# A hybrid encoder trunk on one core: one PSUM ring of four instead of two rings of two, the retention branch put in another order, and column sums issued behind projections

## The chip, the cores and the metric

The kernel runs on 1 core of one Trainium2 chip. The metric is the device time in microseconds of a whole execution, in one launch. Beside it stands the profile of one execution, whose span runs from the first to the last instruction of the program.

## The reference

Two layers (DEPTH = 2) work on 528 tokens (16 learned ones in front of 512) of width 1024, in float32. Each layer does this:

```python
h = h + token_mixer(rms_norm(h, norm_mix[i]), w_in[i], conv_w[i], ...)
h = h + swiglu(rms_norm(h, norm_ffn[i]), w_ffn_in[i], w_ffn_out[i])
```

The mixer projects h by w_in to 12,320 columns and feeds two branches. The gated DeltaNet branch (8 heads of 128) runs a short convolution, normalises q and k, and runs a chunked recurrence in both directions. The retention branch (4 heads, q and k of 256, v of 512) rotates q and k, and adds `gamma^|n-m| (q_n . k_m)` times v over all tokens, forwards and backwards. Each branch's output is divided by its root mean square per head and token, multiplied by a silu gate, and projected up (w_up_a, w_up_b); two sigmoid gates merge them, and w_out gives the mixer's result. The feed-forward part is silu(gate) times up (2816 wide) and a projection back. A last root-mean-square norm drops the 16 learned tokens.

## The kernel before, in words

**Data.** Activations lie with channels on the 128 partitions and tokens along the free axis. Float32 products are made from two reduced-precision parts: a matrix is split into a high and a low tile (`split`, L178: a cast on ScalarE, then a subtraction on VectorE), and `mm3` issues three matmuls for each 128 x 128 block: high x high, high x low, low x high.

**A projection unit** (`project`, L419; `units` calls it and yields) makes 128 output channels: it loads 512 KB of weights on SyncE's DMA queue, splits them, takes PSUM tiles for its token stretches, and issues 24 matmuls for each. In layer 0 the stretches are two of 264 tokens (FULL), so a unit holds two PSUM tiles; in layer 1 many units need only the 512 real tokens (TAIL), one tile. Then `consume` empties each tile on ScalarE or VectorE (a copy for q, k, v; a tanh and a product for gates).

**PSUM** has eight banks of one tile each, in three rings: `pmm` (two, for projection units), `pmx` (two, taken by `pt`, for scores, transposes, products with v, and column sums), and `pmc` (four, taken by `ct`, for the DeltaNet chain and the first units after a norm).

**The mixer.** For each of four pairs of DeltaNet heads, `gdn_begin` makes the projections and convolutions, and `gdn_chain` the recurrence: many small matmuls, each waiting for the step before it on VectorE or ScalarE, and some round trips through DRAM (the tiles nd, w, xd, qc). `weave` (L1042) alternates the steps of the chain with a `filling` generator: three retention heads, gates, and z projections. Each step yields a cost, and `weave` takes as much of the one as of the other by these costs (NA, NB). The fourth retention head comes after all chains (L1075).

**A retention head** (L930) builds a strip of decays, makes q and k (four units, the tiles rp0 and rp1, then the rotation to `rot`), runs other filler, makes the scores of five chunks of keys (`rs` in PSUM, times the strip to `pr`, split to `prh` and `prl`), and then for each of four blocks dv of value channels: one unit for the values (`rvc`), their transposes (`rvt`, `rvm`, split to `rv` and `vst`), one unit for the gate (`rg`), and the product of scores and values (`rpv`: 13 matmuls for each token stretch), emptied by a square (`rsq`) and a product with the gate (`ro`), which goes to DRAM (od_b).

**Column sums of squares** (`mean_square`, L823): two small matmuls with a column of ones (`oms`) for each stretch, on tiles split from the squares (osh and osl of DeltaNet, prh and prl of retention). They are put into the list `later` and given out by `sums`: in the second head's part of `gdn_begin`, ahead of the retention filler, and at the mixer's end. Their rows go to DRAM and come back (`ir`) as inverse roots.

**What follows the mixer** is `project` for w_up_a (emptied by `mrg`), w_up_b, w_out, the feed-forward part, each with weights split on the way. `residual` and `first_units` treat the last and first units at a norm in their own order. In the last layer `done` and `laid` transpose the output (`ops`) as its channels come.

**Order.** The program gives the instructions out in the order of the code; a scheduler at build time then orders each engine's queue by priority, by its own estimate of when each is ready, and by the tiles of a ring that are free (`high_priority` moves some ahead). `issue_after(i)` keeps an instruction behind instruction i on the same engine's queue. On the chip each queue then runs as written. `newest[0]` is the last matmul given out.

Of the kernel before, what the change touches and what calls it, by code (L numbers as in the profile page):

```python
# [9 lines left out]
F32 = mybir.dt.float32  # L10
# [8 lines left out]
P = 128  # L19
# [27 lines left out]
OA = 1000  # L47
OB = 300
UB = 6
TB = 4  # L50

TCKW = dict(schedule_with_timeline_sim=True)
PRI = 200
# [44 lines left out]
def trunk(ctx: ExitStack, tc: tile.TileContext, x, meta, norm_mix, w_in, conv_w, a_log, dt_bias, gdn_norm,  # L98
# [4 lines left out]
    wp = ctx.enter_context(tc.tile_pool(name="wp", bufs=2))  # L103
    xp = ctx.enter_context(tc.tile_pool(name="xp", bufs=1))
    tp = ctx.enter_context(tc.tile_pool(name="tp", bufs=TB))
    pmm = ctx.enter_context(tc.tile_pool(name="pmm", bufs=2, space=PSUM))
    pmx = ctx.enter_context(tc.tile_pool(name="pmx", bufs=2, space=PSUM))
    pmc = ctx.enter_context(tc.tile_pool(name="pmc", bufs=4, space=PSUM))

    newest = [None]  # L110
# [21 lines left out]
        return tp.tile([P, L + 4], F32, name=name, tag="u", bufs=UB)  # L132

    def pt(name="px"):
        return pmx.tile([P, 512], F32, name=name, tag="mx")

    def ct(name="pc"):
        return pmc.tile([P, 512], F32, name=name, tag="mc")
# [163 lines left out]
    with tc.tile_pool(name="ip", bufs=1) as ip:  # L302
        xt = ip.tile([P, NCH, D], F32, name="xt")
        xs_ = ip.tile([P, NCH, D], F32, name="xs")
        raw = tp.tile([42, P], F32, name="gr", tag="t")
        ss = ip.tile([P, NCH], F32, name="ss")
        nc.vector.memset(ss, 1.0)
        act(ss[0:1, 0:1], ss[0:1, 0:1], AF.Square)
        nc.sync.dma_start(xt[0:NM, NC], meta)
        nc.sync.dma_start(xt[:, 0], x[0, 0:P, :])  # L310
        nc.sync.dma_start(xt[:, 1], x[0, P:2 * P, :])
        nc.sync.dma_start(raw[0:16, :], norm_mix.rearrange("l (i p) -> (l i) p", p=P))
        nc.sync.dma_start(raw[16:32, :], norm_ffn.rearrange("l (i p) -> (l i) p", p=P))
        nc.sync.dma_start(raw[32:40, :], norm_final.rearrange("(i p) -> i p", p=P))
        nc.sync.dma_start(raw[40:42, :], gdn_norm)
        ps = pt()
        nc.tensor.transpose(ps[:, :42], raw, ident[:42, :42])
        nc.vector.tensor_copy(gain, ps[:, :42])
        xn = xtiles()
        PARTS = ((NC, 0, 1), (2, 3))  # L320
        warm = pt("warm")
        for _ in range(WU):
            nc.tensor.transpose(warm[:, 0:P], ident, ident)
        SPAN = ((0, 272), (272, 256))

        def turned(i):
            return pmm.tile([P, 512], F32, name="lay", tag="mm") if i % 2 else pt("lay")

        def lay(src, i, part, ps):
            o = 0  # L330
            for c in PARTS[part]:
                n = NM if c == NC else P
                nc.tensor.transpose(ps[:, o:o + n], src[0:n, c, i * P:(i + 1) * P], ident[:n, :n])
                o += n

        def normed(part):
            for c in PARTS[part]:
                n = NM if c == NC else P
                if c == NC:
                    tt(xs_[0:n, c], xt[0:n, c], xt[0:n, c], MUL)  # L340
                    nc.vector.tensor_reduce(out=ss[0:n, c:c + 1], in_=xs_[0:n, c], op=ADD, axis=AX.X)
                else:
                    act(xs_[0:n, c], xt[0:n, c], AF.Square, accum_out=ss[0:n, c:c + 1])
            ms = tp.tile([P, 66], F32, name="ms0", tag="nw", bufs=3)[:, 0:NCH]
            ts(ms, ss, 1.0 / D, MUL, s2=EPS, op2=ADD)
            rs = inverse_root(ms, NCH)
            for c in PARTS[part]:
                n = NM if c == NC else P
                ts(xs_[0:n, c], xt[0:n, c], rs[0:n, c:c + 1], MUL)
            n0, n = SPAN[part]  # L350
            for i in range(KT):
                ps = turned(i)
                lay(xs_, i, part, ps)
                h, lo = xn[0][i][:, n0:n0 + n], xn[1][i][:, n0:n0 + n]
                a = nc.scalar.activation(h, ps[:, :n], AF.Copy, scale=gain[:, i:i + 1])
                b = nc.vector.scalar_tensor_tensor(out=lo, in0=ps[:, :n], scalar=gain[:, i:i + 1], in1=h.bitcast(F32), op0=MUL, op1=SUB)
                if part:
                    behind[:] = a.ins, b.ins

        def before(j):  # L360
            if j == 0:
                for c in (2, 3):
                    nc.sync.dma_start(xt[:, c], x[0, c * P:(c + 1) * P, :])
            normed(j)

        gd = first_gates(0, xn, FULL, before=before, late=True)
# [34 lines left out]
def layer(tc, nc, env, l, xn, gd):  # L401
# [14 lines left out]
    def acc(tiles):  # L416
        return lambda k: tiles[k]

    def project(src, c0, nt, xs, halves, consume, kts=(8,)):  # L419

        xh, xl = xs
        for t in range(nt):
            pss = [pmm.tile([P, 512], F32, name="mmps", tag="mm") for _ in halves]
            k0 = 0
            for j, kt in enumerate(kts):
                w = weights(src[k0 * P:(k0 + kt) * P], c0 + t * P, kt)
                for (n0, n), ps in zip(halves, pss):
                    mm3(ps, w, acc(xh), acc(xl), kt, n0, n, first=j == 0, last=j == len(kts) - 1, k0=k0)
                k0 += kt
            for (n0, n), ps in zip(halves, pss):  # L430
                consume(t, n0, n, ps[:, :n])
# [391 lines left out]
    def mean_square(row, sq, scale, bias, ms, pt):  # L823

        ms = ms[0:1]
        for n0, n in tail:
            ps = pt("oms")
            for j in range(2):
                mm(ps[0:1, :n], one, sq[j][:, n0:n0 + n], start=j == 0, stop=j == 1)
            act(ms[:, n0:n0 + n], ps[0:1, :n], AF.Copy, scale=scale, bias=bias)  # L830
        nc.sync.dma_start(msd[row:row + 1, :], ms[:, t0:L])

# [39 lines left out]
    def gdn_begin(gi, st):  # L872
        hs = (2 * gi, 2 * gi + 1)
        st["ssk"] = gp.tile([P, 2, NCH], F32, name="ssk", tag="ssk")
        nc.vector.memset(st["ssk"], 0.0)
        st["w0"] = gp.tile([68, 1024], F32, name="w0", tag="w0", bufs=1)
        sc = iter(())
        for h in hs:
            for y in gdn_front(h, st):
                next(sc, None)  # L880
                yield y
                if h == hs[1]:
                    sums(ct)
                lead[0] = PRI
            if gi == 0 and h == 0:
                sc = scalars()
                next(sc)
        for _ in sc:
            pass
        sums(ct)  # L890
# [39 lines left out]
    def retention(h, filler):  # L930
# [30 lines left out]
        sums(pt)  # L961
        yield from filler
        pr = []
        for c in range(NCH):
            m0, m = tok(c)
            o = tmp("pr")
            base = 400 - m0
# [10 lines left out]
            else:  # L978
                split(pst[0:NM, t0:L], pst[32:32 + NM, t0:L], o[0:NM, t0:L])
                nc.scalar.copy(pst[64:64 + NM, t0:L], pst[0:NM, t0:L].bitcast(F32))  # L980
            yield 1.8
        sqa = rp.tile([P, SW], F32, name="rsq", tag="strip")[:, 0:L]
        for dv in range(4):
            vc = tmp("rvc")

            def consume(t, n0, n, ps):
                nc.scalar.copy(vc[:, n0:n0 + n], ps)
            yield from units(W, C_VB + h * DV + dv * P, 1, xn, FULL, consume)
            rv = rp.tile([P, 2, NC * P], F32R, name="rv", tag="rot", bufs=2)
            vh, vl = rv[:, 0], rv[:, 1]  # L990
            vst = vsts[dv % 2]
# [6 lines left out]
            nc.tensor.transpose(pm[0:NM, 0:P], vc[:, 0:NM], ident)  # L998
            split(vst[0:NM], vst[64:64 + NM], pm[0:NM, 0:P])
            nc.scalar.copy(vst[32:32 + NM], vst[0:NM].bitcast(F32))  # L1000
            gs = tmp("rg")
            yield from units(W, C_GB + h * DV + dv * P, 1, xn, tail, gated(gs))
            o = tmp("ro")
            sq = sqa if dv == 0 else tmp("rsq2")
            for n0, n in tail:
                ps = pt("rpv")
                for c in range(NC):
                    for a, b in ((vh, 0), (vh, 1), (vl, 0)):
                        mm(ps[:, :n], a[:, c * P:(c + 1) * P], pr[c][b][:, n0:n0 + n], start=c + b == 0 and a is vh, stop=False)
                mm(ps[:, :n], vst, pst[:, n0:n0 + n], start=False)  # L1010
                act(sq[:, n0:n0 + n], ps[:, :n], AF.Square)
                tt(o[:, n0:n0 + n], ps[:, :n], gs[:, n0:n0 + n], MUL)
            nc.sync.dma_start(od_b[h * 4 + dv, :, t0:L], o[:, t0:L])
            if dv:
                tt(sqa[:, t0:L], sqa[:, t0:L], sq[:, t0:L], ADD)
            yield 4.5
        sq = [rp.tile([P, L], F32R, name=n, tag=n, bufs=4) for n in ("prh", "prl")]
        split(sq[0][:, t0:L], sq[1][:, t0:L], sqa[:, t0:L])
        later.append(lambda ps: mean_square(H + h, sq, 4.0 / DV, 4 * 256 * EPS, tmp("ms"), ps))

    def merge_gates(i0, i1):
# [54 lines left out]
        pass  # L1076
    sums(pt)
    mixctx.close()

    bctx = ExitStack()  # L1080
    b0 = bctx.enter_context(tc.tile_pool(name=f"b0{l}", bufs=1, reuse_waits="tile"))
# [186 lines left out]
    def done(i, h, n0, n):  # L1268
# [8 lines left out]
        if i == 7 and n0 > NM:  # L1277
            laid(i, h, n0, n)
            finish(n0, n)
        elif i < 7:  # L1280
            laid(i, h, n0, n)
        else:
            half.append((i, h, n0, n))

    half = []

# [49 lines left out]
```

## Time and profile before

| | us |
|---|---|
| median of 3 runs | 2948.24 (2946.37 to 2952.17) |
| the profiled execution | 2948.52 |
| its span | 2946.7 |
| PE busy in it | 2831.8 |
| DVE busy | 1802.9 |
| ACT busy | 1103.0 |

PE is TensorE's matmul stream, PEld its weight loads, DVE VectorE, ACT ScalarE. Busy time is the union of an engine's instructions. The projections (tile mmps) hold most of it. The mixer of layer 0 runs to about 915 us and its dense part to 1503 us; the mixer of layer 1 runs from about 1530 to 2385 us.

### The profile page before, as it was taken

The numbers are of one execution on the slowest core, as the hardware profiler recorded it, in microseconds if no ns is written. First come the engines' busy times: TensorE is split into PE (matmuls) and PEld (weight loads), VectorE is DVE, ScalarE is ACT, GpSimd is POOL, SyncE is SP. The second block draws the span as 40 slices with busy tenths as digits, with TensorE's granted clock in tenths as the row PEclk, the third lists the DMA queues.
The fourth block names the chain that finished last, engine by engine and source line by source line (L and its number), as shares of the span: only waits on it lengthen the run. The fifth ranks groups of instructions, "written<-read, shape, count | busy, mean of one in ns | idle before, by whom it ended". The sixth has DMA issues, their size and how long they took to land.

```text
span 2946.7 us, 48876 instructions
## 1 busy us (share of the span) xinstructions
PE 2831.8 (96%) x19487; PEld 2574.8 (87%) x19487; DVE 1802.9 (61%) x3854; ACT 1103.0 (37%) x2171; POOL 9.0 (0%) x114
## 2 busy tenths in 40 slices
PE   8999999999989999999999899999999999999998
PEld 8899998899979999999998797887888778888887
DVE  6867968778565445433358768687785654543333
ACT  5434444344333233222244343443444332332222
POOL 0000000000000000000000000000000000000000
PEclk9999999999999999999999999999999999999999
DMA  6322323234345442333444323334243464433332
GB/s 165 104 80 77 105 77 105 73 78 118 87 147 167 128 142 84 89 93 95 120 116 109 103 68 96 87 83 108 70 118 94 144 188 121 127 108 98 94 107 81
DMA packets 506423, 313.49 MB, mean 106 GB/s; under 512 B 55632, under 2 KB 460778, under 8 KB 506194
## 3 DMA queue, kind: packets, MB, share of 16 engines
q1 hardware_dynamic: 506194, 310.36, 37.1%
q8 instruction: 153, 2.51, 0.4%
q14 instruction: 76, 0.62, 0.1%
HBM read 265.28 MB, written 45.02 MB: 105 GB/s over the span
## 4 chain that ended last, share of the span: by engine, by line
PE 80%; DVE 10%; DMA 6%; ACT 3%; issue 1%; SPq 1%; DVEq 0%; ACTq 0%
PE mmps L113 64%; PE rpv L113 3%; PE oo L113 2%; PE fu L113 1%; DVE wlo L180 1%; PE rs L113 1%; PE sn L113 1%; PE yy L113 1%; DMA lo<-od_a 1%; ACT whi L179 1%; PE ks L113 1%; DMA xd<-w 1%; DVE N L116 1%; DMA gcr<-grow 1%; DMA nd<-NT 1%
## 5 line engine op out<-in xcount | busy, mean ns | idle before, releaser
L113 PE MATMUL mmps<-xh,whi 128*128 128x264 f32 (+1 forms) x3840 | 1195.8, 312 | 24.2 <-ACT rp L946 12.3
L113 PE MATMUL mmps<-xl,whi 128*128 128x264 f32 (+1 forms) x3840 | 1184.9, 309 | 0.0
L113 PE MATMUL mmps<-xh,wlo 128*128 128x264 f32 (+1 forms) x3808 | 1178.6, 310 | 0.5 <-DVE wlo L180 0.5
L113 PEld LDWEIGHTS mmps<-xh,whi 128*128 128x128 f32 x3840 | 730.0, 190 | 69.2 <-ACT rp L946 13.6
L113 PEld LDWEIGHTS mmps<-xl,whi 128*128 128x128 f32 x3840 | 729.3, 190 | 38.3 <-issue 4.0
L113 PEld LDWEIGHTS mmps<-xh,wlo 128*128 128x128 f32 x3808 | 722.6, 190 | 36.8 <-issue 2.3
L180 DVE TENSOR_TENSOR wlo<-wraw,whi 128x1024 fp32r<-128x1024 f32 (+1 forms) x392 | 474.4, 1211 | 457.4 <-ACT whi L179 455.1
L179 ACT CAST whi<-wraw 128x1024 fp32r<-128x1024 f32 (+1 forms) x392 | 408.3, 1042 | 888.9 <-PE mmps L113 667.6
L113 PE MATMUL mmps<-oh,whi 128*128 128x264 f32 (+2 forms) x1126 | 359.2, 319 | 7.2 <-DVE mrg L116 7.0
L113 PE MATMUL mmps<-ol,whi 128*128 128x264 f32 (+2 forms) x1126 | 358.4, 318 | 0.0
L113 PE MATMUL mmps<-oh,wlo 128*128 128x264 f32 (+2 forms) x1126 | 358.0, 318 | 0.0
L113 PEld LDWEIGHTS mmps<-oh,whi 128*128 128x128 f32 x1126 | 211.7, 188 | 24.1 <-DVE mrg L116 5.5
L113 PEld LDWEIGHTS mmps<-oh,wlo 128*128 128x128 f32 x1126 | 211.9, 188 | 15.7
L113 PEld LDWEIGHTS mmps<-ol,whi 128*128 128x128 f32 x1126 | 211.7, 188 | 15.2
L116 DVE SCALAR_TENSOR_TENSOR ac<-xc,cw,ac 128x528 f32<-128x528 f32 x192 | 146.4, 763 | 6.9 <-ACT ac L126 1.4
L119 DVE TENSOR_TENSOR ff<-fg,mmps 128x264 f32<-128x264 f32 (+1 forms) x63 | 32.4, 515 | 115.7 <-PE mmps L113 115.7
L113 PE MATMUL rpv<-prh,rv 128*128 128x264 f32 (+1 forms) x384 | 96.0, 324 | 1.7 <-DVE rv L180 1.7
L113 PE MATMUL rs<-rot 128*128 128x264 f32 (+3 forms) x240 | 82.2, 475 | 11.5 <-DVE pr L119 8.7
L119 DVE TENSOR_TENSOR st<-w 68x30 f32<-68x30 f32 (+14 forms) x240 | 78.2, 326 | 23.1 <-DMA w<-ndm 10.3
L126 ACT ACTIVATE gth<-mmps 128x264 f32<-128x264 f32 (+1 forms) x132 | 60.0, 454 | 61.1 <-PE mmps L113 61.0
L119 DVE TENSOR_TENSOR w<-w,st 68x30 f32<-68x30 f32 (+14 forms) x240 | 78.1, 326 | 6.7
L116 DVE SCALAR_TENSOR_TENSOR hn<-mmps,hold 128x264 f32<-128x264 f32 (+2 forms) x51 | 25.3, 498 | 76.9 <-PE mmps L113 70.9
(315 smaller groups left out, 3191.6 us busy)
## 6 DMA issues: line engine op xcount, KB each, us to landing
wraw<-in_w_in_dram SPq DMA_DIRECT2D x194, 512.0 KB
wraw<-in_w_ffn_in_dram SPq DMA_DIRECT2D x88, 512.0 KB
wraw<-in_w_up_b_dram SPq DMA_DIRECT2D x32, 512.0 KB
wraw<-in_w_ffn_out_dram SPq DMA_DIRECT2D x32, 512.0 KB
gcr<-grow SPq DMA_DIRECT2D x32, 264.0 KB
wraw<-in_w_up_a_dram SPq DMA_DIRECT2D x16, 512.0 KB
wraw<-in_w_out_dram SPq DMA_DIRECT2D x16, 512.0 KB
wraw<-in_w_ffn_out_dram SPq DMA_DIRECT2D x16, 384.0 KB
```

The source lines that it names most:

```text
L113: newest[0] = nc.tensor.matmul(o, lhsT=l, rhs=r, start=start, stop=stop)
L116: (eng or nc.vector).scalar_tensor_tensor(out=o, in0=a, scalar=s, in1=b, op0=op0, op1=op1)
L119: (eng or nc.vector).tensor_tensor(out=o, in0=a, in1=b, op=op)
L126: nc.scalar.activation(o, a, f, **kw)
L179: a = nc.scalar.copy(hi, src)
L180: return a.ins, nc.vector.tensor_tensor(out=lo, in0=src, in1=hi.bitcast(F32), op=SUB).ins
```

## The change

- The rings `pmm` and `pmx` become one ring of four (`pmm`), from which both `project` and `pt` take tiles; `turned` takes all of its tiles from it.
- After a layer's mixer (`wide[0] = 1`) `project` takes the tiles of one unit from `pmc` and those of the next from `pmm` in turn.
- A retention head gives out its value unit and its gate unit for block 0 among the scores (after chunks 1 and 3), and then, for each block, the values of block dv, the product of block dv - 1, the transposes of block dv, and the gate of block dv. The cost that a product yields is 3.2 and not 4.5.
- `mean_square` keeps its matmuls behind the newest matmul given out, and `gdn_begin` gives out the sums one step later.
- In the last layer `done` transposes a block when the next has come, the pool of temporary tiles `t` has six places and not four, and the DMA scratch size is 1024 and not 2048.

```diff
--- before.py
+++ after.py
@@ -47,7 +47,7 @@
 OA = 1000
 OB = 300
 UB = 6
-TB = 4
+TB = 6
 
 TCKW = dict(schedule_with_timeline_sim=True)
 PRI = 200
@@ -103,8 +103,7 @@
     wp = ctx.enter_context(tc.tile_pool(name="wp", bufs=2))
     xp = ctx.enter_context(tc.tile_pool(name="xp", bufs=1))
     tp = ctx.enter_context(tc.tile_pool(name="tp", bufs=TB))
-    pmm = ctx.enter_context(tc.tile_pool(name="pmm", bufs=2, space=PSUM))
-    pmx = ctx.enter_context(tc.tile_pool(name="pmx", bufs=2, space=PSUM))
+    pmm = ctx.enter_context(tc.tile_pool(name="pmm", bufs=4, space=PSUM))
     pmc = ctx.enter_context(tc.tile_pool(name="pmc", bufs=4, space=PSUM))
 
     newest = [None]
@@ -132,7 +131,7 @@
         return tp.tile([P, L + 4], F32, name=name, tag="u", bufs=UB)
 
     def pt(name="px"):
-        return pmx.tile([P, 512], F32, name=name, tag="mx")
+        return pmm.tile([P, 512], F32, name=name, tag="mm")
 
     def ct(name="pc"):
         return pmc.tile([P, 512], F32, name=name, tag="mc")
@@ -324,7 +323,7 @@
         SPAN = ((0, 272), (272, 256))
 
         def turned(i):
-            return pmm.tile([P, 512], F32, name="lay", tag="mm") if i % 2 else pt("lay")
+            return pt("lay")
 
         def lay(src, i, part, ps):
             o = 0
@@ -416,11 +415,15 @@
     def acc(tiles):
         return lambda k: tiles[k]
 
+
+    wide = [0]
+
     def project(src, c0, nt, xs, halves, consume, kts=(8,)):
 
         xh, xl = xs
         for t in range(nt):
-            pss = [pmm.tile([P, 512], F32, name="mmps", tag="mm") for _ in halves]
+            wide[0] += wide[0] > 0
+            pss = [(ct if wide[0] % 2 else pt)("mmps") for _ in halves]
             k0 = 0
             for j, kt in enumerate(kts):
                 w = weights(src[k0 * P:(k0 + kt) * P], c0 + t * P, kt)
@@ -825,8 +828,9 @@
         ms = ms[0:1]
         for n0, n in tail:
             ps = pt("oms")
-            for j in range(2):
-                mm(ps[0:1, :n], one, sq[j][:, n0:n0 + n], start=j == 0, stop=j == 1)
+            with tc.issue_after(newest[0].ins):
+                for j in range(2):
+                    mm(ps[0:1, :n], one, sq[j][:, n0:n0 + n], start=j == 0, stop=j == 1)
             act(ms[:, n0:n0 + n], ps[0:1, :n], AF.Copy, scale=scale, bias=bias)
         nc.sync.dma_start(msd[row:row + 1, :], ms[:, t0:L])
 
@@ -875,12 +879,15 @@
         nc.vector.memset(st["ssk"], 0.0)
         st["w0"] = gp.tile([68, 1024], F32, name="w0", tag="w0", bufs=1)
         sc = iter(())
+        turns = 0
         for h in hs:
             for y in gdn_front(h, st):
                 next(sc, None)
                 yield y
                 if h == hs[1]:
-                    sums(ct)
+                    turns += 1
+                    if turns > 1:
+                        sums(ct)
                 lead[0] = PRI
             if gi == 0 and h == 0:
                 sc = scalars()
@@ -961,7 +968,8 @@
         sums(pt)
         yield from filler
         pr = []
-        for c in range(NCH):
+
+        def scores(c):
             m0, m = tok(c)
             o = tmp("pr")
             base = 400 - m0
@@ -978,14 +986,23 @@
             else:
                 split(pst[0:NM, t0:L], pst[32:32 + NM, t0:L], o[0:NM, t0:L])
                 nc.scalar.copy(pst[64:64 + NM, t0:L], pst[0:NM, t0:L].bitcast(F32))
-            yield 1.8
-        sqa = rp.tile([P, SW], F32, name="rsq", tag="strip")[:, 0:L]
-        for dv in range(4):
-            vc = tmp("rvc")
+
+        V, G, S = {}, {}, []
+
+        def values(dv):
+            V[dv] = tmp("rvc")
 
             def consume(t, n0, n, ps):
-                nc.scalar.copy(vc[:, n0:n0 + n], ps)
+                nc.scalar.copy(V[dv][:, n0:n0 + n], ps)
             yield from units(W, C_VB + h * DV + dv * P, 1, xn, FULL, consume)
+
+        def gates(dv):
+            G[dv] = tmp("rg")
+            yield from units(W, C_GB + h * DV + dv * P, 1, xn, tail, gated(G[dv]))
+
+        def turn(dv):
+
+            vc = V[dv]
             rv = rp.tile([P, 2, NC * P], F32R, name="rv", tag="rot", bufs=2)
             vh, vl = rv[:, 0], rv[:, 1]
             vst = vsts[dv % 2]
@@ -998,10 +1015,13 @@
             nc.tensor.transpose(pm[0:NM, 0:P], vc[:, 0:NM], ident)
             split(vst[0:NM], vst[64:64 + NM], pm[0:NM, 0:P])
             nc.scalar.copy(vst[32:32 + NM], vst[0:NM].bitcast(F32))
-            gs = tmp("rg")
-            yield from units(W, C_GB + h * DV + dv * P, 1, xn, tail, gated(gs))
+            V[dv] = vh, vl, vst
+
+        def weighted(dv):
+            vh, vl, vst = V[dv]
             o = tmp("ro")
-            sq = sqa if dv == 0 else tmp("rsq2")
+            sq = tmp("rsq2") if S else rp.tile([P, SW], F32, name="rsq", tag="strip")[:, 0:L]
+            S.append(sq)
             for n0, n in tail:
                 ps = pt("rpv")
                 for c in range(NC):
@@ -1009,13 +1029,30 @@
                         mm(ps[:, :n], a[:, c * P:(c + 1) * P], pr[c][b][:, n0:n0 + n], start=c + b == 0 and a is vh, stop=False)
                 mm(ps[:, :n], vst, pst[:, n0:n0 + n], start=False)
                 act(sq[:, n0:n0 + n], ps[:, :n], AF.Square)
-                tt(o[:, n0:n0 + n], ps[:, :n], gs[:, n0:n0 + n], MUL)
+                tt(o[:, n0:n0 + n], ps[:, :n], G[dv][:, n0:n0 + n], MUL)
             nc.sync.dma_start(od_b[h * 4 + dv, :, t0:L], o[:, t0:L])
             if dv:
-                tt(sqa[:, t0:L], sqa[:, t0:L], sq[:, t0:L], ADD)
-            yield 4.5
+                tt(S[0][:, t0:L], S[0][:, t0:L], sq[:, t0:L], ADD)
+
+
+        for c in range(NCH):
+            scores(c)
+            yield 1.8
+            if c == 1:
+                yield from values(0)
+            if c == 3:
+                yield from gates(0)
+        turn(0)
+        for dv in range(1, 5):
+            if dv < 4:
+                yield from values(dv)
+            weighted(dv - 1)
+            yield 3.2
+            if dv < 4:
+                turn(dv)
+                yield from gates(dv)
         sq = [rp.tile([P, L], F32R, name=n, tag=n, bufs=4) for n in ("prh", "prl")]
-        split(sq[0][:, t0:L], sq[1][:, t0:L], sqa[:, t0:L])
+        split(sq[0][:, t0:L], sq[1][:, t0:L], S[0][:, t0:L])
         later.append(lambda ps: mean_square(H + h, sq, 4.0 / DV, 4 * 256 * EPS, tmp("ms"), ps))
 
     def merge_gates(i0, i1):
@@ -1076,6 +1113,7 @@
         pass
     sums(pt)
     mixctx.close()
+    wide[0] = 1
 
     bctx = ExitStack()
     b0 = bctx.enter_context(tc.tile_pool(name=f"b0{l}", bufs=1, reuse_waits="tile"))
@@ -1277,10 +1315,10 @@
         if i == 7 and n0 > NM:
             laid(i, h, n0, n)
             finish(n0, n)
-        elif i < 7:
-            laid(i, h, n0, n)
-        else:
-            half.append((i, h, n0, n))
+            return
+        while half:
+            laid(*half.pop())
+        half.append((i, h, n0, n))
 
     half = []
 
@@ -1322,7 +1360,7 @@
     import concourse.bacc as bacc
     from concourse.bass_utils import run_bass_kernel_spmd as run
 
-    nc = bacc.Bacc("TRN2", target_bir_lowering=False, num_devices=1, dynamic_dma_scratch_size=2048)
+    nc = bacc.Bacc("TRN2", target_bir_lowering=False, num_devices=1, dynamic_dma_scratch_size=1024)
     arrays, args = {}, []
     given = [(n, np.ascontiguousarray(inputs[n])) for n in _INS] + [("const", CONST)]
     for name, a in given:
```

## Rows read from the trace of the kernel before

**Rows 1.** The page: busy time, share of the span and instructions of each engine.

```profile
PE 2831.8 (96%) x19487; PEld 2574.8 (87%) x19487; DVE 1802.9 (61%) x3854; ACT 1103.0 (37%) x2171; POOL 9.0 (0%) x114
```

**Rows 2.** Both mixers: window, length, busy of PE, PEld, DVE, ACT, POOL; clock; DMA.

```profile
65.00:925.00 860.00, 819.28 (x6510) 778.57 (x6509) 623.69 (x1508) 361.45 (x832) 3.19 (x44) 0.98 0.35 96
...
1590.00:2310.00 720.00, 684.78 (x4388) 589.55 (x4387) 536.86 (x1299) 304.97 (x666) 2.89 (x40) 0.99 0.34 91
```

**Rows 3.** The chain that ended last, dense stretch: start, length, what.

```profile
1139.04 363.74 PE mmps L113 x2978
```

**Rows 4.** Who waited for whom, PE: total, times, longest.

```profile
PE mmps L113 <- ACT rp L946: 12.3, 6, 4.8
...
PE rs L113 <- DVE pr L119: 8.7, 6, 3.5
PE lvy L113 <- DVE QT L119: 8.1, 5, 3.5
...
PE rvt L995 <- ACT rvc L987: 7.1, 6, 1.7
PE mmps L113 <- DVE mrg L116: 7.0, 3, 2.4
PE mmps L113 <- ACT xc L538: 6.8, 9, 1.5
PE oms L113 <- ACT osh L179: 6.5, 7, 2.2
PE mmps L113 <- DVE rg L116: 3.5, 4, 1.7
PE rvt L995 <- DVE w L119: 3.1, 1, 3.1
...
PE oms L113 <- ACT prh L179: 2.7, 1, 2.7
PE oms L113 <- DVE prl L180: 1.8, 3, 0.9
PE rpv L113 <- DVE rv L180: 1.7, 3, 0.8
PE oms L113 <- DVE osl L180: 1.6, 4, 0.4
```

**Rows 5.** ACT in order of time at the longest projection wait: start, length, instruction.

```profile
517.14 0.98 ACT L126 ACTIVATE strip<-strip 128x928 f32<-128x928 f32 x1 [9.41 <-DVE strip L116]
518.02 0.36 ACT L946 COPY rp<-mmps 128x264 f32<-128x264 f32 x1
```

**Rows 6.** Products emptied, slowest and last case: start, length, instruction.

```profile
190.59 0.29 PE L113 MATMUL rpv<-pst,vst 96*128 96x264 f32 x1
...
195.69 0.43 DVE L119 TENSOR_TENSOR ro<-rpv,rg 128x264 f32<-128x264 f32 x1
...
910.26 0.29 PE L113 MATMUL rpv<-pst,vst 96*128 96x264 f32 x1
...
911.01 0.43 DVE L119 TENSOR_TENSOR ro<-rpv,rg 128x264 f32<-128x264 f32 x1 [0.21 <-ACT rsq L126]
```

**Rows 7.** Who waited for whom, DVE for DMA: total, times, longest.

```profile
DVE qd L683 <- DMA qc<-xd: 26.3, 7, 5.3
...
DVE dm L116 <- DMA gcr<-grow: 12.6, 12, 1.9
...
DVE st L119 <- DMA w<-ndm: 10.3, 6, 3.8
```

**Rows 8.** Column sums at the last chain's end, each layer: busy, mean ns, idle before.

```profile
L113 PE MATMUL oms<-osh,one 128*1 128x264 f32 x4 | 1.0, 342 | 2.4 <-ACT osh L179 2.4
...
L113 PE MATMUL oms<-osh,one 128*1 128x512 f32 x2 | 0.8, 392 | 2.4 <-ACT osh L179 2.4
```

**Rows 9.** ACT's q and k copies; the issue of DMAs: nanoseconds least, median, most.

```profile
L946 ACT COPY rp<-mmps 128x264 f32<-128x264 f32 (+1 forms) x56 | 22.3, 404 | 40.9 <-PE mmps L113 19.3 <-issue 18.3 <-DMA od_b<-ro 3.2
...
L1013 SPq DMA_DIRECT2D od_b<-ro x32: 319/339/417, 161.8 to 2379.6; - x32
```

## The prediction

> **What bounds the kernel now.** I read the page first: PE is busy 2831.8 of the 2946.7 us span, 96% [rows 1], so the time is PE's stream and its holes. The stages come next. In the dense part of layer 0 the chain of waits shows 2978 projection matmuls in 363.74 us, 0.122 us each, with no hole [rows 3]; more banks can give nothing there. In the mixers PE stands idle for 860.0 - 819.3 = 40.7 us (layer 0) and 720.0 - 684.8 = 35.2 us (layer 1), while ACT and DVE are far from full [rows 2]. The holes are therefore waits of an in-order queue, not work, and the third view, who PE waited for, names them [rows 4]: PSUM tiles not yet emptied (rp, xc, rg, mrg, pr), values not yet copied (rvc, rv), column sums whose squares are late (oms), and steps of the DeltaNet chain (lvy and smaller ones). The change leaves every instruction on PE, ACT, DVE and the DMA queues as it is in kind and number; it moves them. So the sum is one of waits, made against the profiled execution (2948.52 us, of which 1.8 lie outside the span), which is within 0.3 us of the median shown.
>
> **The change part by part.**
>
> *One ring of four, inside the mixers.* A unit of 264 + 264 tokens holds two tiles, and before there were only two, so the next unit's first half waited for the last one's to be copied. At the longest such wait ACT stood 9.41 us at the strip's exponential, and the copy of rp stood behind it in ACT's queue [rows 5]. With four tiles PE can run one more unit, 48 x 0.122 = 5.9 us, which is more than the longest of these waits (4.8). The waits for rp and xc are 12.3 + 6.8 and that for rg is 3.5, 22.6 in all [rows 4]. I take 17 off, since a unit ahead also needs its weights split by the same ACT and DVE. Bounds: 0 (the same queue is late for the next tile as well) and 22.6. Part of the rp wait comes from temporaries: 3.2 us of the idle time before those copies on ACT ended with the DMA that frees ro [rows 9]. Six places for four cover that; it is inside the 17.
>
> *What the shared ring costs.* In layer 0 a block now asks for eight tiles in this order: values 2, product 2, transposes 2, gate 2. The gate's first half takes the place of the product's first half, four tiles back. Between the two lie the product's second half (13 x 0.122 = 1.6 us) and five transposes, which I estimate at the same 0.122 us each (0.6 us): 2.2 us in which the square and ro must be done. Before, the stretch from the product's last matmul to the end of ro ran from 0.89 us (190.59 and 910.26 are the slowest and the last case; 911.01 + 0.43 - 910.55) to 5.24 us [rows 6]. Of the 16 first halves in layer 0 five are above 2.2, by 7.8 us together. Three of four blocks are followed by a gate, so I take +6. Bounds: 0, and 12 x 3.1 = 37 if every block is like the slowest. In layer 1 the product and the gate take one tile each, and the place that falls due has been empty for a whole unit, so nothing there.
>
> *After the mixer, projections over both rings.* PE waited 7.0 us for mrg, three times, at most 2.4 us [rows 4]. Eight tiles are more than enough: 6.5 off. Bounds 0 and 7.0. The rest of that part has no wait for a tile to give back [rows 3].
>
> *Scores among projections.* The scores waited 8.7 us for pr, which empties their two tiles on DVE [rows 4]. With units between and four tiles I take two thirds, 5.8. Bounds: 8.7 off, and the loss worked out under the third rival.
>
> *Value products a block late.* The transposes used to follow their own values at once and waited 7.1 us for the copy rvc (at most 1.7) and 3.1 once for a DVE queue stuck on a DMA; the product waited 1.7 for rv [rows 4]. Now a product of 26 x 0.122 = 3.2 us stands between values and transposes, and a gate unit and a value unit between transposes and product. Both waits for copies are covered: 8.8 off, and 1 of the 3.1. Bounds 0 and 11.9. What is late next is ro, priced above.
>
> *Column sums behind the newest projection.* PE waited 6.5 + 2.7 + 1.8 + 1.6 = 12.6 us for the squares or their split [rows 4]. Given out after a projection, most sums find them ready. But at the end of the fourth chain of each layer the newest matmul given out is a retention unit that has long run, and 2.4 + 2.4 us of the waits stand just there [rows 8]; these stay. Of the other 7.8 I take 6. Bounds 0 and 7.8. Behind a sum queue the copy ms on ACT and a DMA; their rows are read much later, as the inverse roots are wanted only after the mixer. For the last sum of a mixer nothing changes, since the newest matmul is its own head's product.
>
> *At nothing:* the later transposes of the output, `turned`, and the smaller DMA scratch. The transposes go from one place to a later one between dense projections. A DMA's issue takes 0.34 us in the median and 0.42 at most on a queue that is off PE's path [rows 9]; twice that would still be hidden by weights loaded units ahead, and if that cover went it would show as waits for whi or wlo. Bounds: 1 us either way.
>
> *New waits.* PE reaches the DeltaNet steps earlier when projections stop waiting, and some of the time given back turns into waits for the chain. The nearest row is lvy's 8.1 us [rows 4]; I take +6, with bounds 0 and 15 (about its double).
>
> Sum: -17 + 6 - 6.5 - 5.8 - 9.8 - 6 + 6 = -33.1, which makes 2948.5 - 33 = 2915 us, 1.1% less.
>
> **The rivals.**
>
> *The banks are not what holds PE.* ACT and DVE, late for one tile, would be late for its neighbours too, and only the reordering pays: the sum without the first and the mrg term (23.5) is -9.6, so 2939. For it: the longest rp wait came from one blocked ACT queue that also splits weights [rows 5]. Against it: each such wait is shorter than the one unit that the new ring adds. Beside this stands the Trainium skill, "TensorE: Matmul & The Clock Gate", section "HAM oscillation — how this bites in real kernels": there a second set of PSUM buffers "gave no further gain" for one kernel. By that this rival would hold; the waits for rp, xc and mrg [rows 4] speak against it here.
>
> *All of it goes.* Every wait addressed vanishes and nothing takes its place: 22.6 + 7.0 + 8.7 + 11.9 + 7.8 = 58.0, so 2890. For it: many of these waits are below 2 us. Against it: the ring's own price, and a chain with steps of its own.
>
> *DVE stops block the projections (slower).* DVE stands in its queue for DMAs of the chain: 26.3 us for qc, 12.6 for gcr and 10.3 for w, 49.2 in all [rows 7]. Before, tiles that wait for DVE (rs, the transposes, the products) could fill only their own two places, and units emptied by ACT went on in theirs. In one ring four such tiles can stop every projection. If all of these stops reach PE, the time is 2948.5 - 33 + 49 = 2965; it is slower from the point at which two thirds of them do (33 of 49). For it: the slowest product was emptied 5.24 us late [rows 6]. Against it: most stops are short (12 of them share 12.6 us), and the new order puts units between the tiles that need DVE.
>
> **How the numbers follow.** Chances: the forecast 0.50 (its own range 2900 to 2930), banks don't matter 0.16, all goes 0.14, DVE stops 0.20. The range is 2888 to 2958: it holds the forecast and the first rival, about half of the second, and the milder half of the third, so some 0.17 is left out. A difference of 0.2% (5.9 us) is about what a measurement of this kernel can tell from none. Faster by more: 0.50 + 0.14 + 0.09 of the first rival = 0.73. Within it: 0.06 of the first and 0.02 of the third rival = 0.08. Slower: 0.18 of the third and 0.01 of the first = 0.19.
>
> **What would show it.** In the changed kernel's list of PE's waits the lines for rp, xc, mrg and rvc should be nearly gone and that for pr cut to a third; a new line "mmps for ro" of about 6 us should stand there, in layer 0 alone; the oms line should be near 5 us, at two places, the ends of the last chains. PE's idle time in the mixers should fall from 76 us to about 50. The dense part should still take 0.122 us a matmul. The forecast is wrong if PE's work itself grows, if the waits for the chain (lvy, sn, yy) grow by more than 15 us, or if waits for pr or ro in front of projections come to more than the gains.

## The result and the profile after

The changed kernel takes 2925.27 us (median of 5, 2914.74 to 2931.79) against 2948.24: a ratio of 0.9915 (95% interval 0.989 to 0.994), so 23 us less by the medians and 25 by the ratio. Its profiled execution took 2931.79 us, span 2930.0, and is the slowest of the five; traces are compared span with span, 16.7 us less than before.

The page answers [rows 1]: the same 19487 instructions, PE busy 2.6 us less.

```profile
PE 2829.2 (97%) x19487; PEld 2586.1 (88%) x19487; DVE 1796.7 (61%) x3854; ACT 1101.9 (38%) x2171; POOL 9.0 (0%) x114
```

The windows answer [rows 2]; the last two are the hole described below and the stretch from it to the end of the fourth chain.

```profile
65.00:925.00 860.00, 824.42 (x6568) 788.24 (x6567) 624.71 (x1513) 364.84 (x833) 3.17 (x44) 0.98 0.35 97
1590.00:2310.00 720.00, 687.28 (x4377) 593.07 (x4376) 544.99 (x1307) 310.03 (x675) 2.88 (x40) 0.97 0.36 99
2209.70:2221.00 11.30, 0.64 (x3) 0.20 (x2) 6.57 (x14) 5.03 (x14) 0.00 (x0) 0.74 0.40 87
2209.70:2268.60 58.90, 42.74 (x270) 37.76 (x268) 31.01 (x89) 18.98 (x60) 0.00 (x0) 0.71 0.08 18
```

PE's idle time is 35.6 us in layer 0 and 32.7 in layer 1, 68.3 together; it was 75.9, and about 50 was forecast. The dense chain of layer 0 is as it was [rows 3], 0.122 us a matmul:

```profile
1131.96 363.94 PE mmps L112 x2982
```

Who waited for whom on PE (total, times, longest), for [rows 4]:

```profile
PE lvy L112 <- DVE QT L118: 19.4, 7, 10.7
PE mmps L112 <- DVE rg L115: 12.7, 8, 4.5
...
PE oms L112 <- ACT osh L178: 6.1, 6, 2.2
PE mmps L112 <- ACT xc L541: 5.3, 5, 1.5
PE mmps L112 <- DVE ro L118: 4.9, 2, 3.5
...
PE oms L112 <- DVE osl L179: 2.7, 6, 0.5
PE rvm L1015 <- DVE pr L118: 2.5, 1, 2.5
PE lvt L112 <- DVE Y L118: 2.4, 3, 0.8
...
PE mmps L112 <- ACT rp L953: 1.3, 1, 1.3
...
PE mmps L112 <- DVE pr L118: 0.6, 1, 0.6
```

The lines for mrg, rvc, rv and w are gone, rp is down from 12.3 to 1.3, and pr from 8.7 to 0.6 and the 2.5 of rvm. All PE waits together fell only from 105.3 to 91.6 us: lvy grew from 8.1 to 19.4 and rg from 3.5 to 12.7, and ro is new. More than half of lvy is one hole. The chain of waits around it:

```profile
2207.79 6.24 DMA xd<-w
...
2214.46 2.25 DMA qc<-xd
...
2220.80 2.09 PE lvy L112 x8
```

The steps of layer 1's fourth DeltaNet chain had to go through DRAM (xd, qc). After the matmul that starts at 2209.75 the next ones in PE's queue are steps of this chain, so PE has 0.64 us of work in 11.3. In the hole the granted clock fell to 1.2 GHz. The chain's own small matmuls are slower there, as the groups of PE for 2195 to 2300 us show (busy, mean ns, idle before); the second row answers [rows 8], and 2.2 us of the 2.4 have stayed:

```profile
L112 PE MATMUL lvy<-QT,N 128*128 128x128 f32 x16 | 4.2, 441 | 13.7 <-DVE QT L118 13.7
...
L112 PE MATMUL oms<-osh,one 128*1 128x512 f32 x2 | 0.8, 390 | 2.2 <-ACT osh L178 2.2
```

DVE's waits for DMAs [rows 7] are shorter (26.3 and 12.6 before), and the one for w fell from 10.3 to 7.5, so those stops did not become a bound on PSUM tiles in general; the hole above is a stop of the chain itself, for xd and qc:

```profile
DVE qd L686 <- DMA qc<-xd: 23.6, 6, 6.3
...
DVE dm L115 <- DMA gcr<-grow: 5.6, 10, 1.0
```

One of them still did what the third rival describes. In order of time (start, length, instruction, idle time): the product ends at 377.4, ACT stands 5.26 us for qc with the product's square behind it, DVE waits for ACT with ro behind that, and the gate's unit waits 3.47 us for its place. It is the counterpart of [rows 6].

```profile
377.14 0.29 PE L112 MATMUL rpv<-pst,vst 96*128 96x264 f32 x1
...
381.54 0.30 ACT L690 COPY qd<-qc 128x128 f32<-128x128 f32 x1 [5.26 <-DMA qc<-xd]
...
383.89 0.43 DVE L118 TENSOR_TENSOR ro<-rpv,rg 128x264 f32<-128x264 f32 x1
...
384.37 0.39 PE L112 MATMUL mmps<-xh,whi 128*128 128x264 f32 x1 [3.47 <-DVE ro L118]
```

The copies of rp no longer wait for a DMA, as their group on ACT shows [rows 9]:

```profile
L953 ACT COPY rp<-mmps 128x264 f32<-128x264 f32 (+1 forms) x56 | 21.8, 404 | 28.8 <-PE mmps L112 22.2 <-issue 6.4 <-DVE rot L118 0.2
```

### The profile page after: what moved, and what is told of

Read it like the earlier page. It is cut to its first block, busy times and chain, and to the rows that moved or that the text cites. A ratio compares the mean times of both kernels' runs of the same rounds, so it can differ in the third digit from the quotient of the medians.

```text
span 2930.0 us, 48768 instructions
## 1 busy us (share of the span) xinstructions
PE 2829.2 (97%) x19487; PEld 2586.1 (88%) x19487; DVE 1796.7 (61%) x3854; ACT 1101.9 (38%) x2171; POOL 9.0 (0%) x114
## 4 chain that ended last, share of the span: by engine, by line
PE 84%; DVE 7%; DMA 5%; ACT 2%; issue 1%; SPq 0%; DVEq 0%; ACTq 0%
PE mmps L112 66%; PE rpv L112 3%; PE fu L112 2%; PE oo L112 2%; PE sn L112 1%; DMA xd<-w 1%; DVE wlo L179 1%; PE yy L112 1%; DMA lo<-od_a 1%; PE ks L112 1%; PE rs L112 1%; PE lvy L112 1%; PE lvt L112 1%; ACT whi L178 1%; PE lvq L112 1%
## 5 line engine op out<-in xcount | busy, mean ns | idle before, releaser
L112 PE MATMUL mmps<-xh,whi 128*128 128x264 f32 (+1 forms) x3840 | 1188.4, 310 | 25.4 <-DVE rg L115 12.7
L112 PE MATMUL rs<-rot 128*128 128x264 f32 (+3 forms) x240 | 74.6, 456 | 2.8 <-DVE z L115 2.8
```

What stands on the lines that cost most here:

```text
L112: newest[0] = nc.tensor.matmul(o, lhsT=l, rhs=r, start=start, stop=stop)
```

## The experiments

Times are medians and ratios are to the kernel before, run on the same chip; that kernel's medians lay between 2949.5 and 2951.4 us. The order here is not that of the runs: the parts taken out of the changed kernel (two rings, old body, old sums, pace) ran first, and the expectations of the others refer to them. First, parts put onto the kernel before. The letters in the expectations are those of the theories named there.

**Temporaries alone.** Six places for t and the smaller DMA scratch.

```diff
-TB = 4
+TB = 6
```

> The kernel before with only six places for temporaries in place of four (and the smaller DMA scratch that makes the room). Undoing the ring, the order or the sums one at a time cost nothing that can be told from 2925 us, so either two of them cover for one another or the gain has another source. Theory A (waits for tiles, values and sums, each covered by more than one part): 2941 to 2949 us, since in the trace of before only 3.2 us of a wait ended with the freeing of a temporary. Theory D, the temporaries are the source: 2922 to 2932 us, with the waits for rp and pr gone though both rings have two tiles.

2951.14 us, 1.0001 (0.9992 to 1.0009): no effect.

**The ring alone.**

```diff
-    pmm = ... bufs=2 ...
-    pmx = ... bufs=2 ...
+    pmm = ... bufs=4 ...
     def pt(name="px"):
-        return pmx.tile(...)
+        return pmm.tile(...)
```

> The kernel before with only the one ring of four (four temporaries, old order, old sums, no turns after the mixer). Theory A: the waits of projections for rp, xc and rg (22.6 us) fall below 8 us, the time to 2930 to 2938 us. The rival that the banks don't matter, and theory D: 2943 to 2951 us.

2959.75 us, 1.0031 (1.0019 to 1.0043): slower, which neither expectation had. PE's waits of this kernel:

```profile
PE rpv L112 <- ACT rv L178: 17.9, 12, 3.0
PE ops L1289 <- ACT hn L125: 16.9, 8, 2.2
```

The second line is the last layer's output. Its transposes need hn, which DVE and then ACT make from the projection just ended. Before, they waited in their own ring and the next projection passed; in one ring they hold the place in front of it. PE in order of time, one of the eight:

```profile
2829.48 0.40 PE L112 MATMUL mmps<-oh,wlo 128*128 128x512 f32 x1
2832.08 0.66 PE L1289 MATMUL ops<-c_ident,hn 128*128 128x128 f32 x4 [2.20 <-ACT hn L125]
```

**The ring and the later output transposes.** As above, with the changed `done`.

```diff
+        while half:
+            laid(*half.pop())
+        half.append((i, h, n0, n))
```

> The kernel before with the one ring of four and with the output's transposes one block later, as in the changed kernel; four temporaries, old order, old sums, no turns. Theory G: the ring alone was slower only because the transposes (ops) waited eight times for their block's copy, 16.9 us, and the projections behind them could not pass; the mixers gained. Then these waits go and the time is 2935 to 2943 us. If the ring brings nothing in the mixers: 2946 to 2952 us.

2937.17 us, 0.9958 (0.9945 to 0.9972). The deferral is worth some 22 us against the ring alone (22.6 by the medians), and the last stage is 24.7 us shorter (387.7 for 412.4): it takes away a stall that the ring itself brings. The waits for hn are 15.4 us of that; the clock record also has 17 us at 1.2 GHz among the transposes of the ring alone (2813 to 2933 us) and none here. What is left is a gain of 12 to 14 us, with rp nearly gone and a new wait of the product for rv, the split of the transposed values:

```profile
PE rpv L112 <- ACT rv L178: 17.8, 12, 2.8
...
PE ops L1289 <- ACT hn L125: 1.5, 1, 1.5
...
PE mmps L112 <- ACT rp L945: 1.3, 1, 1.3
```

**The order alone.** The new retention body on the two old rings, with six temporaries.

```diff
+        turn(0)
+        for dv in range(1, 5):
+            if dv < 4:
+                yield from values(dv)
+            weighted(dv - 1)
...
```

> The kernel before with the new order inside a retention head and six temporaries; two rings of two, old sums, no turns after the mixer. Theory A: waits for rvc, rv and pr (17.5 us) fall below 6, the time to 2930 to 2938 us. Theory D: the same time as six temporaries alone, within 5 us.

2938.13 us, 0.9955 (0.9941 to 0.9968), 12 to 13 us less. It gains as much as the ring does, and it too takes rp away, without another bank; here lvy, at 17.8, is what replaces it:

```profile
PE lvy L113 <- DVE QT L119: 17.8, 9, 3.8
...
PE mmps L113 <- ACT rp L946: 1.3, 3, 0.8
```

Now parts taken out of the changed kernel.

**Two rings of two again**, everything else kept (`project` takes turns between `ct` and the old `pmm`).

```diff
-    pmm = ... bufs=4 ...
+    pmm = ... bufs=2 ...
+    pmx = ... bufs=2 ...
```

> The changed kernel with the two PSUM rings of two again (projections from the one, scores, transposes, products and sums from the other; after the mixer projections still go to the ring of four in turn). Theory A, tiles: the waits of projections for rp and xc come back (6.6 us in the changed kernel, 19.1 before), those for rg and ro (17.6) shrink below 8; on balance 0 to 10 us slower than the changed kernel's 2925 us. Theory B, the banks don't matter: 2925 within 5 us. Theory C, the shared ring costs more than it gives: rg and ro go and little comes back, 2910 to 2918 us.

2927.25 us, 0.9921 (0.9908 to 0.9935): level with the changed kernel (0.9915). On top of the order and the turns the ring gives nothing that can be measured: rp and xc come back in part, z is new (6.5), lvy (12.4) and rg (3.9) shrink, and ro is gone.

```profile
PE mmps L113 <- ACT xc L542: 8.6, 7, 1.5
...
PE mmps L113 <- ACT rp L954: 6.4, 4, 2.3
```

**The old retention body**, with its old cost of 4.5, everything else kept.

```diff
-        for dv in range(1, 5):
-            if dv < 4:
-                yield from values(dv)
-            weighted(dv - 1)
...
+        for dv in range(4):
+            vc = tmp("rvc")
...
```

> The changed kernel with the old order inside a retention head (scores, then values, transposes, gate and product of one block after the other). Theory A: waits for rvc, rv and pr come back (about 15 us), those for rg and ro go (17.6): 2925 to 2938 us. Theory B, the order is the whole gain: 2943 to 2950 us.

2925.0 us, 0.9916 (0.9902 to 0.9929): level again. On top of the ring and the turns the order gives nothing either. Its waits are those of the ring alone: 16.6 us for rv and 6.0 for pr, with rp, rg and ro gone.

**Without the turns.**

```diff
-    wide[0] = 1
```

> The changed kernel without the turns between the two rings after the mixer (projections there stay in the one ring of four). Undoing the ring, the order or the sums cost 3 us at most, and the order alone brought 12 of the 25 us, so 11 are left for turns and sums. Theory E, the turns carry them: 2931 to 2938 us, with waits for mrg, hn or ol back after the mixer. Theory F, the ring of four is enough there: 2925 within 4 us.

2936.3 us, 0.9956 (0.9944 to 0.9969), so the turns carry about 11 us; the two pairs that differ mainly by them agree (2938.13 to 2927.25, and 2937.17 to 2925.0). Ring and order together, with the sums and no turns, thus gain no more than either alone. Their waits show one that neither makes alone: projections wait 13.8 us for rg here, 0.9 with the order alone, and 0.3 with the ring and the later output transposes (the last row):

```profile
PE mmps L112 <- DVE rg L115: 13.8, 8, 4.9
...
PE oms L112 <- ACT prh L178: 4.9, 2, 2.7
```

```profile
PE mmps L112 <- DVE rg L115: 0.3, 1, 0.3
```

The time of theory E came, but not its waits. There is no line for mrg in this run, nor in the two with the ring alone on the kernel before: the ring of four takes mrg away without the turns. (On two rings the turns do it: mrg is 8.6 us with the order alone, and gone with two rings and turns.) What the turns change here stands at the mixers' ends. Without turns PE's queue has the last sums in front of the next projections, waits for their squares, and runs at 1.2 GHz soon after (0.22 us a matmul from 909.7):

```profile
907.98 0.28 PE L112 MATMUL oms<-prh,one 128*1 128x264 f32 x1 [2.22 <-ACT prh L178]
...
909.09 0.28 PE L112 MATMUL mmps<-oh,whi 128*128 128x264 f32 x1
...
909.95 0.42 PE L112 MATMUL mmps<-oh,whi 128*128 128x264 f32 x1
```

The two ends cost 5.4 us in waits (prh 4.9, prl 0.5) and have 6.8 us at 1.2 GHz in the clock record, which at half speed can cost 3.4 more; the changed kernel has neither. The rest of the 11 us was not traced. With turns, the changed kernel goes from the last product straight into w_up_a:

```profile
908.48 0.28 PE L112 MATMUL rpv<-pst,vst 96*128 96x264 f32 x1
908.60 0.28 PE L112 MATMUL mmps<-oh,whi 128*128 128x264 f32 x1
```

**The old place of the sums**: no `issue_after`, and given out at the old step.

```diff
-                    if turns > 1:
+                    if turns > 0:
...
-            with tc.issue_after(newest[0].ins):
```

> The changed kernel with the column sums given out as before (not held behind the newest matmul, and one step earlier in a pair of heads). Theory A: PE's waits for the squares rise from 8.8 to about 13 us and the time by 3 to 8 us, 2928 to 2933. Theory B, the waits only change their place: 2925 within 4 us.

2927.74 us, 0.9921 (0.9909 to 0.9934). The waits for oms even shrink to 5.6 + 1.2. The time differs by 2.5 us, which is inside the intervals: the sums' part is not told from none, and its sign stays open.

**The pace.** The product yields its old cost.

```diff
-            yield 3.2
+            yield 4.5
```

> The changed kernel with the product's yielded cost back at 4.5 (3.2 in the changed kernel), nothing else. Theory A, pacing: the smaller cost makes each of the first three chains take about 4 us more filler, so that the fourth runs out of it and PE waits 10.7 us for lvy at 2210 us and stands on half clock after it. Then PE's waits for lvy fall from 19.4 to below 10 us and the time to 2910 to 2918 us. Theory B, blocking: the filler that is left (gates, scores, values of the fourth retention head) can't go ahead because the column sums of the last two DeltaNet heads stand in front of it for their tiles. Then the long wait stays (15 us or more for lvy) and the time is 2925 within 6 us.

2924.08 us, 0.9912 (0.9899 to 0.9926). The longest wait for lvy falls from 10.7 to 3.4 us, but lvy sums to 15.8 and the time is the same: here the pace moved where the chain starves, and little else.

Last, the filler itself. The sums of the last two DeltaNet heads stand ahead of the fourth retention head's scores, though they need the end of the chain and the scores do not.

**Late rows.** These sums go behind the scores; nothing else differs from the changed kernel.

```diff
-        sums(pt)
+        sums(pt, h == 3)
...
         for c in range(NCH):
             scores(c)
...
+        sums(pt)
         turn(0)
```

`sums(pt, True)` keeps the DeltaNet items in `later`; the head's last two merge gates (`filler`) stand between the two places, so they too go ahead of the sums.

> The changed kernel, with the column sums of the last two DeltaNet heads given out after the fourth retention head's scores and not before its last two merge gates. Theory B of the pacing run (the filler that is left stands behind these sums): gates, scores and the first value and gate units go on PE while the fourth chain runs, the 10.7 us wait for lvy shrinks to under 4 and the oms wait at the chain's end goes; 2905 to 2917 us. If the filler is simply used up, or is held by something else: 2925 within 5 us.

2884.7 us (2880.99 to 2885.85), 0.9777 (0.9764 to 0.979): 40 us below the changed kernel, more than the 8 to 20 that were expected. The scores of layer 1's fourth head (count, duration, first and last start), first in the changed kernel, then with late rows:

```profile
L112 PE MATMUL rs<-rot x20: 590/592/602, 2282.8 to 2302.5; 128*128 128x512 f32 x16, 128*16 128x512 f32 x4
```

```profile
L112 PE MATMUL rs<-rot x20: 590/592/697, 2204.8 to 2230.2; 128*128 128x512 f32 x16, 128*16 128x512 f32 x4
```

They start 78 us earlier, in among the steps of the last chain, as the chain of waits shows (start, length, what):

```profile
2204.96 0.86 PE rs L112 x2
2205.82 0.89 PE lvy L112 x8
2206.70 2.58 PE rs L112 x6
```

The window from the place of the hole to the chain's end, then lvy's group for 2195 to 2300 us, then the waits:

```profile
2209.70:2261.00 51.30, 49.95 (x341) 41.55 (x339) 31.52 (x85) 19.80 (x56) 0.00 (x0) 0.90 0.14 38
```

```profile
L112 PE MATMUL lvy<-QT,N 128*128 128x128 f32 x16 | 2.1, 274 | 0.0
```

```profile
PE mmps L112 <- DVE ro L118: 9.5, 4, 3.1
...
PE mmps L112 <- DVE rg L115: 6.5, 6, 1.5
...
PE lvy L112 <- DVE QT L118: 2.8, 3, 1.3
```

From 2209.7 to the chain's end PE is busy 49.95 of 51.3 us and not 42.74 of 58.9, the mean granted clock is 0.90 and not 0.71, and lvy runs at 274 ns and not 441. Over the whole kernel PE's idle time falls by 25.7 us and its busy time, with the same instructions, by 21.0: in the trace's clock record 40.0 us of the span lie at 1.2 GHz where 97.1 did. (These two sum to 46.7 us and not to 40, as the changed kernel's profile is of its slowest execution.) Layer 0 does the same on a smaller scale (its mixer is 14 us shorter, layer 1's 29).

**Late rows on the kernel before.**

```diff
-        sums(pt)
+        sums(pt, h == 3)
```

> The kernel before with only the column sums of the last two DeltaNet heads given out after the fourth retention head's scores. If what blocks there was in the kernel before already and is apart from the change: 30 to 42 us faster than before, 2908 to 2920 us, as with the changed kernel (40 us). If the shared ring and the new order made it worse, or are needed to use the room: 5 to 20 us faster, 2930 to 2945 us.

2947.92 us, 0.9989 (0.998 to 0.9998): some 3 us, and neither expectation. The scores do go ahead, from 2297.5 us to 2265.7. But in the old body values and gates come only after the scores, so they are now behind the sums: the first copy of values is at 2305.7, behind the sums' copies (2304.7), while late rows on the changed kernel has it at 2214.0. There is also less to fill, since the longest wait for lvy is 3.5 us there. So the gain needs more of the change; by the queue it is the new order, but late rows were not run on the order alone.

**Gate first**, on top of late rows: the gate's unit ahead of the transposes.

```diff
             if dv < 4:
-                turn(dv)
                 yield from gates(dv)
+                turn(dv)
```

> The changed kernel with those column sums late (2884.7 us) and with the gate unit of a block before its transposes, so that the place that the gate takes is that of the values, copied long ago, and the transposes take that of the product 5.9 us after it. If the waits for ro and rg in front of projections (9.5 and 6.5 us) are the ring's price for the place four tiles back: they fall below 5 together and the time to 2871 to 2880 us. If they come from late DVE whatever the place: 2885 within 4 us.

2911.45 us, 0.987 (0.9856 to 0.9884): a miss. The wait for ro (9.5) goes as intended, but against late rows 26.8 us are lost: rg doubles from 6.5, and the products wait for gates and values.

```profile
PE mmps L112 <- DVE rg L115: 14.3, 10, 3.2
...
PE rpv L112 <- DVE rg L115: 3.6, 2, 2.6
PE rpv L112 <- ACT rv L178: 3.6, 4, 1.1
```

With ro gone these rows add 5.5 us (7.8 + 7.2 - 9.5); in all, PE's waits grow by 19 us (66.2 to 85.2), over a dozen lines, and its busy time by 6.7. Why was not traced to one place.

## Why the prediction was right, and which of its terms were not

The forecast of 2915 us was 10 us too low, inside its own range of 2900 to 2930; the sum of -33 should have been -23. That it came so near is in part luck: ring and order in the mixers brought half of what was summed for them, and the turns nearly twice their term, for another reason than the one given.

*Adding the ring to the order.* This step failed. The ring in the mixers with its price (-17 + 6), the values (-9.8) and the scores (-5.8) came to -26.6 as if they were separate. Each half alone does about half of that (12 to 13 us less for the order, 12 to 14 for the ring with later output transposes), and both with the sums, without turns, do 13 to 15. The waits show two reasons. Both remove the same rp waits [rows 4]: with either, rp is 1.3. And only the two together make projections wait for rg (13.8 us without turns, 12.7 with, against 0.9 and 0.3) and for ro (4.9). How much of the missing 12 us each of the two reasons holds was not separated. Of the 22.6 us in the ring's account rp gave 11.0, xc only 1.5, and rg grew. Three waits for xc of 1.49 us each were there before and are still there with four tiles; the one looked at, at 1742.9 us, stands in ACT's queue behind squares of the chain's output and the copies of k and v.

*The price of the ring.* Forecast +6, as a wait for ro in layer 0 alone: it is 4.9, in layer 0 alone. Missed was rg, +9.2, 7.5 of its 12.7 us in layer 1, where I had put nothing. (The five first halves above 2.2 us exceed it by 7.6 us in the trace, not 7.8; the term does not hang on it.)

*The turns.* Forecast -6.5, measured -11. mrg went, but not by them: with the ring of four it is gone without the turns too, so the 6.5 belonged to the ring. What the turns gave was elsewhere. "For the last sum of a mixer nothing changes" was wrong: the turns let w_up_a pass it.

*Scores and values.* By their waits both were right: pr lost 5.6 with the 2.5 of rvm counted (forecast 5.8), and rvc, rv and w are gone (11.9, forecast 9.8). That this did not arrive in the time is the first point's overlap.

*Sums.* oms fell by 3.8 (forecast 6), and 2.2 and 2.3 us stay for osh at the last chains' ends, as forecast; in time nothing that can be told from none.

*New chain waits.* Forecast +6, at most 15: lvy +11.3 and lvt +1.6, so within the bound and twice the value. The low clock behind the one long hole was not in the sum at all.

*At nothing.* For temporaries and scratch that was measured. For the later output transposes the number came out, but the reason given was wrong: they are not free, they save some 22 us that the ring would cost.

*The rivals.* "All of it goes" missed. "DVE stops" shows its mechanism once, at 3.5 us, by way of ACT. "The banks are not what holds PE" gives 2939, and the order alone does measure 2938, but the banks alone, with later output transposes, measure 2937, so its reason fails. The Trainium skill, "TensorE: Matmul & The Clock Gate", section "HAM oscillation — how this bites in real kernels", reports "no further gain" from a second set of PSUM buffers: here that holds on top of the new order (2927.25 with two rings, 2925.27 with one) and not on top of the old one (0.9958).

## What to carry to other kernels

When two edits remove the same wait, try each alone before adding their gains, and look for a wait that only the two together make: here two gains of about 13 us made 13 to 15. When the waits that you took away come back as waits for a serial chain, look for what lies behind that chain's end in the queue without needing it; moving such filler forward was worth more on top of the change (40 us) than the change itself (23 us), and only 3 us without it. Before rings are joined, list who holds a place while it waits, and for whom.

## What the runs showed that I had not expected

In the profiled execution a single hole is dearer than its length. In the 10.66 us before lvy the granted clock fell to 1.2 GHz, at 2215.1 by the trace's clock record, and it stayed there for 34.1 of the 37.5 us to 2252.6 (stretches of 13.7 and 20.5 us), although PE had matmuls again from 2220.8; the 128 x 128 matmuls of lvy took 441 ns on average there and 274 ns with late rows. But taking this hole away did not pay by itself: with the old pace no wait for lvy is above 3.4 us, lvy's matmuls take 274 ns there, 59.6 us of the span lie at 1.2 GHz where 97.1 did, and the time is the same. The profiled execution is the slowest of the five, so how long the hole is in the others is not known.

How far executions differ also changed: the five of the changed kernel spread over 17 us, the four with late rows over 5. Whether the hole causes that spread was not tested; the kernel without turns has the same hole (10.5 us) and five executions within 2.4 us, which speaks against it.
